# Norms through a constant matrix, single tiles in the first stage, and narrow work between pieces of a product

## The chip, the core and the metric

The kernel runs on one core of a Trainium2 chip. The metric is the device time of one execution: 1261.98 us is the median of three runs (1261.39 to 1262.31). TensorE multiplies matrices into PSUM. VectorE (DVE), ScalarE (ACT) and GpSimd (POOL) do elementwise work. SyncE (SP) issues most transfers.

## The reference

One layer for 320 rows (256 of a prompt, 64 of a running stream), width 2048, in float32:

```
h = RMSNorm(x);  z = h @ w_in            # 2048 -> 1024 q, 128 k, 128 v, 1024 u, 1024 v of the gate
q, k = per-head RMSNorm;  a = windowed attention(q, k, v), 16 heads, bias table, sinks
s = u * (W_s RMSNorm(gelu(zv)) + b), u = gelu(zu)
x = x + concat(RMSNorm(a), RMSNorm(s)) @ w_out       # 2048 -> 2048
y = x + square(relu(RMSNorm(x) @ w_up)) @ w_down      # 2048 -> 8192 -> 2048
```

## The kernel before

Activations lie transposed: 128 features on the partitions, the 320 rows as columns (`T`), so a product takes 128 x 128 blocks of weights as stationary and 320 columns as moving operand. To keep float32 accuracy each operand is split into two fp32r halves, and three passes are added: `w_hi` with `XH`, `w_hi` with `XL`, `w_lo` with `XH`. ScalarE copies a loaded piece of weights into `w_hi` (L125), VectorE subtracts to get `w_lo` (L126). A piece holds 4 tiles of 128 rows by 256 columns, 512 KB, and gives 24 "wide" matmuls (L136). A product is 256 output columns: four pieces for 2048 rows, 96 wide matmuls, into one of two accumulators (`acc`, `ps_acc` with two buffers). The whole program has 8160 wide matmuls. `w_raw` has three buffers in `wp`; from `w_out` on it has seven, in the pool `wf`, which is opened where the pool `at` (attention's tiles) is closed (L455) and takes its memory. `w_hi` and `w_lo` have three buffers each.

A norm's factor is applied after the product, at the eviction from PSUM, so a product can start before its norm is known. The factor is made by `rstd_rows` and `spread`: squares are added up over the tiles, three f32 matmuls sum over the partitions (L158; an f32 matmul runs as two halves in the trace), VectorE adds eps, GpSimd takes the power, three f32 matmuls spread the factors over the partitions (L169) and VectorE copies them out.

The first stage (`products` with `first`) computes two products side by side, keys and values (`kv_ps`, in `acc`) and the first queries (`q0_ps`), as x and weights arrive: single tiles of 128 rows for tiles 0 to 3, then three blocks of four. Each step loads x, splits it into `XH` and `XL` (L178, L179), and loads and splits two weight blocks; only the first four tiles are pinned to program order. Then come three products of queries, four of v with attention's ten units (`attend`) between, four of u, and `w_out` in two halves of eight products (half 0 over attention's output `AH`, `AL`, half 1 over the gate's), and the feed-forward part. The order on each engine is set by a scheduler from program order and its own view of when things are ready; `tc.issue_after` puts an instruction behind another, `keep_in_program_order` pins it. SP's loads follow each other in program order (`load`); small transfers in `between` (the bias) go four at a time behind a load.

Of the kernel before, what the change touches and what calls it, by code (L numbers as in the profile page):

```python
# [29 lines left out]
def hymba_step_kernel(ctx: ExitStack, tc: tile.TileContext, i, o):  # L30
# [47 lines left out]
    inv_dm = const.tile([P, 1], F32, name="inv_dm")  # L78
    nc.vector.memset(inv_dm, 1.0 / DM)
    inv_1k = const.tile([P, 1], F32, name="inv_1k")  # L80
    nc.vector.memset(inv_1k, 1.0 / 1024)
    hone = const.tile([P, 2], F32, name="hone")
# [3 lines left out]
    hsel = const.tile([P, 2], F32, name="hsel")  # L86
    nc.vector.memset(hsel, 0.0)
    nc.vector.memset(hsel[0:HD, 0:1], 1.0 / HD)
    nc.vector.memset(hsel[HD:P, 1:2], 1.0 / HD)


    loads, between, steps = [], [], []
# [8 lines left out]
    def chunks(n, first):  # L101
        if first:
            return [(a, 1) for a in range(4)] + [(a, 4) for a in range(4, n, 4)]
        return [(a, 4) for a in range(0, n, 4)]

    def products(w, k0, nk, jobs, rh, rl, first=None, deep=None):


        wv = w.rearrange("(kt p) n -> p kt n", p=P)
        steps.clear()  # L110
        for a, n in chunks(nk, first is not None):
            if first is not None:
                first(a, n)
                if a % 4 == 0:
                    ahead = blk("w_first", [P, len(jobs), 4, 256])
            for j, (c0, ps) in enumerate(jobs):
                if first is not None:
                    raw = ahead[:, j, a % 4:a % 4 + n]
                else:
                    raw = (deep or wp).tile([P, 4, 256], F32, name="w_raw", tag="w_raw")  # L120
                hi = wp.tile([P, 4, 256], F32R, name="w_hi", tag="w_hi", bufs=3)
                lo = wp.tile([P, 4, 256], F32R, name="w_lo", tag="w_lo", bufs=3)
                load(raw[:, :n], wv[:, k0 + a:k0 + a + n, c0:c0 + 256])
                pin = tc.keep_in_program_order if first is not None and a < 4 else lambda ins: ins
                high = pin(nc.scalar.activation(out=hi[:, :n], in_=raw[:, :n], func=AF.Copy))  # L125
                low = pin(nc.vector.tensor_tensor(out=lo[:, :n], in0=raw[:, :n], in1=hi[:, :n].bitcast(F32),  # L126
                                                  op=ALU.subtract))
                tail = isinstance(ps, list) and a + n == nk
                kgs = [(k, g) for g in range(2) for k in range(n)] if tail else [(k, g) for k in range(n) for g in range(2)]
                passes = [(w_, r_, x) for x, (w_, r_) in enumerate(((hi, rh), (hi, rl), (lo, rh)))]  # L130

                for (k, g), (w_, r_, x) in [(kg, p_) for p_ in passes for kg in kgs] if first is not None else \
                        [(kg, p_) for kg in kgs for p_ in passes]:
                    kk = a + k
                    out = ps[g][:, 0:T] if isinstance(ps, list) else ps[:, g, 0:T]
                    mm = nc.tensor.matmul(out=out, lhsT=w_[:, k, g * P:(g + 1) * P], rhs=r_(kk),  # L136
                                          start=(kk == 0 and x == 0), stop=(kk == nk - 1 and x == 2))
                steps.append((high.ins, low.ins, mm.ins))

    def sums(name):  # L140

        t = sm.tile([P, TP], F32, name=name, tag="ssq", bufs=2)
        nc.gpsimd.memset(t[:, T:TP], 0.0)
        return t
# [4 lines left out]
    def product(w, k0, nk, c0, rh, rl, deep=None, apart=False):  # L149
        ps = [misc(), misc()] if apart else acc_tile()  # L150
        products(w, k0, nk, [(c0, ps)], rh, rl, deep=deep)
        return ps

    def rstd_rows(sq, weight, eps, h=1):

        st = misc()
        for t in range(3):
            nc.tensor.matmul(out=st[:, t * h:t * h + h], lhsT=sq[:, t * P:(t + 1) * P], rhs=weight, start=True, stop=True)  # L158
        r = sm.tile([P, 3 * h], F32, name="r_rows", tag="r_rows")
        nc.vector.tensor_scalar(out=r, in0=st[:, 0:3 * h], scalar1=eps, scalar2=None, op0=ALU.add)  # L160
        rs = sm.tile([P, 3 * h], F32, name="rs_rows", tag="rs_rows")
        nc.gpsimd.tensor_tensor(out=rs, in0=r, in1=nhalf[:, 0:3 * h], op=ALU.pow)
        return rs

    def spread(rs, name):
# [5 lines left out]
        out = sm.tile([P, T], F32, name=name, tag="rstd_b", bufs=2)  # L171
        nc.vector.tensor_copy(out=out, in_=bc[:, 0:T])
        return out

# [9 lines left out]
    def load_x(a, n):  # L184
        load(xT[:, a:a + n], xv[:, a:a + n])
        for k in range(a, a + n):
            split(xT[:, k], g_mix[:, k:k + 1], XH[:, k], XL[:, k], pinned=a < 4)
# [8 lines left out]
    products(w_in, 0, KT, [(1024, kv_ps), (0, q0_ps)], xh, xl, first=load_x)  # L196

    kvx = blk("kvx", [P, 1152])
    kn = kvx[:, 0:448]
    vT = kvx[:, 448:768]  # L200
    rkx = kvx[:, 768:1152].rearrange("p (t c) -> p t c", t=3)
# [13 lines left out]
    nc.sync.dma_start(out=sgb.rearrange("p g i -> p (g i)"), in_=i["sgu_b"].to_broadcast([P, 1024]))  # L215
    wsT = at.tile([P, 8, P], F32, name="wsT", bufs=1)
    nc.sync.dma_start(out=wsT, in_=i["sgu_wT"])
    nc.gpsimd.memset(wsT[HD:P, :, 0:HD], 0.0)
# [3 lines left out]
    b_ps = misc()  # L222
    with tc.issue_after(steps[9][2]):
        nc.tensor.matmul(out=b_ps[0:16, 0:255], lhsT=tab, rhs=oneh, start=True, stop=True)
    b_row = sm.tile([16, 255], F32, name="b_row", tag="w1", bufs=3)
    nc.vector.tensor_copy(out=b_row, in_=b_ps[0:16, 0:255])
    b_dram = dram.tile([16, 15, 255], F32, name="b_dram")
    nc.gpsimd.dma_start(out=b_dram, in_=b_row[:, None, :].to_broadcast([16, 15, 255]))
# [8 lines left out]


    ssq2 = sm.tile([P, 2, T], F32, name="ssq2", tag="w2", bufs=4)
    for k in range(0, KT, 2):  # L240
        sq = sm.tile([P, 2, T], F32, name="sq2", tag="w2", bufs=4) if k else ssq2
        with tc.issue_after(steps[9][0]):
            nc.scalar.activation(out=sq, in_=xT[:, k:k + 2], func=AF.Square)
# [3 lines left out]
    nc.vector.tensor_tensor(out=ssq[:, 0:T], in0=ssq2[:, 0], in1=ssq2[:, 1], op=ALU.add)  # L247

    rx = spread(rstd_rows(ssq, inv_dm, EPS), "rx")


    zk = sm.tile([P, T], F32, name="zk", tag="w2", bufs=4)
    nc.vector.tensor_tensor(out=zk, in0=kv_ps[:, 0, 0:T], in1=rx, op=ALU.mult)
    nc.vector.tensor_tensor(out=vT, in0=kv_ps[:, 1, 0:T], in1=rx, op=ALU.mult)
    sq = sums("ksq")
    nc.scalar.activation(out=sq[:, 0:T], in_=zk, func=AF.Square)
    rk = rstd_rows(sq, hsel, EPS, 2)
# [3 lines left out]
    def queries(g, q_ps):  # L261
# [6 lines left out]
        nc.scalar.activation(out=sq, in_=qg, func=AF.Square)  # L268
        st = misc()
        for b in range(5):  # L270
            nc.tensor.matmul(out=st[:, 2 * b:2 * b + 2], lhsT=sq[:, b].rearrange("p a t -> p (a t)"), rhs=hone,  # L271
                             start=True, stop=True)
# [30 lines left out]
    for g in range(1, 4):  # L303
        queries(g, product(w_in, 0, KT, g * 256, xh, xl))
# [263 lines left out]
```

## Time and profile before

| | us |
|---|---|
| median of the runs | 1261.98 |
| profiled execution | 1262.67 |
| its span, first to last instruction | 1260.9 |
| TensorE busy | 1251.8 |
| VectorE, ScalarE, GpSimd busy | 635.5, 488.9, 104.1 |

"Busy" is the time in which an engine had an instruction running. A matmul's row shows its own length (309 ns), but matmuls overlap, so their pace is read from a stretch of the chain of waits, divided by the count. An instruction's bracket gives the idle time of its engine just before it and what ended that.

### The profile page before, as it was taken

The numbers are of one execution on the slowest core, as the hardware profiler recorded it, in microseconds if no ns is written. First come the engines' busy times: TensorE is split into PE (matmuls) and PEld (weight loads), VectorE is DVE, ScalarE is ACT, GpSimd is POOL, SyncE is SP. The second block draws the span as 40 slices with busy tenths as digits, with TensorE's granted clock in tenths as the row PEclk, the third lists the DMA queues.
The fourth block names the chain that finished last, engine by engine and source line by source line (L and its number), as shares of the span: only waits on it lengthen the run. The fifth ranks groups of instructions, "written<-read, shape, count | busy, mean of one in ns | idle before, by whom it ended". The sixth has DMA issues, their size and how long they took to land.

```text
span 1260.9 us, 20260 instructions
## 1 busy us (share of the span) xinstructions
PE 1251.8 (99%) x8559; PEld 1238.0 (98%) x8559; DVE 635.5 (50%) x731; ACT 488.9 (39%) x636; POOL 104.1 (8%) x100
## 2 busy tenths in 40 slices
PE   8999999999999999999999999999999999999998
PEld 7998899999999999999999999999999999999998
DVE  6547857756864444444444444344444334444443
ACT  7335546523543342233333333344333333343221
POOL 1213443400310000000000000000000000000000
PEclk8999999999999999999999999999999999999999
DMA  9553334644445544445544444555444444544550
GB/s 281 168 141 106 97 115 125 213 142 147 148 143 150 151 149 150 150 149 151 151 150 151 151 150 151 151 150 150 151 150 150 145 149 149 150 152 160 170 168 32
DMA packets 186427, 187.79 MB, mean 149 GB/s; under 512 B 6464, under 2 KB 185856, under 8 KB 186336
## 3 DMA queue, kind: packets, MB, share of 16 engines
q1 hardware_dynamic: 185696, 185.43, 47.5%
q0 software_dynamic: 496, 1.03, 0.4%
q8 instruction: 67, 1.10, 0.4%
q14 instruction: 24, 0.20, 0.0%
q10 hardware_dynamic: 144, 0.03, 0.0%
HBM read 182.91 MB, written 3.32 MB: 148 GB/s over the span
## 4 chain that ended last, share of the span: by engine, by line
PE 98%; DMA 1%; SPq 0%; ACT 0%; POOL 0%; issue 0%; DVE 0%; POOLq 0%
PE acc L136 93%; PE misc L136 1%; PE q_ps L136 1%; DMA xT<-in_xT 1%; PE misc L365 1%; PE misc L371 1%; PE s_ps L327 1%; SPq L99 0%; PE misc L271 0%; PE misc L427 0%; PE misc L158 0%; POOL s L355 0%; PE misc L419 0%; PE misc L169 0%; PE misc L428 0%
## 5 line engine op out<-in xcount | busy, mean ns | idle before, releaser
L126 DVE TENSOR_TENSOR w_lo<-w_raw,w_hi 128x1024 fp32r<-128x1024 f32 x332 | 413.0, 1244 | 458.8 <-ACT w_hi L125 449.8
L125 ACT ACTIVATE w_hi<-w_raw 128x1024 fp32r<-128x1024 f32 x332 | 351.8, 1060 | 714.2 <-PE acc L136 675.7
L136 PE MATMUL acc<-H2H,w_hi 128*128 128x320 f32 x1024 | 316.6, 309 | 0.0
L136 PE MATMUL acc<-H2L,w_hi 128*128 128x320 f32 x1024 | 316.4, 309 | 0.0
L136 PE MATMUL acc<-H2H,w_lo 128*128 128x320 f32 x1024 | 316.4, 309 | 0.0
L136 PE MATMUL acc<-FH,w_hi 128*128 128x320 f32 x992 | 306.5, 309 | 0.0
L136 PE MATMUL acc<-FL,w_hi 128*128 128x320 f32 x992 | 306.5, 309 | 0.0
L136 PE MATMUL acc<-FH,w_lo 128*128 128x320 f32 x992 | 306.5, 309 | 0.0
L136 PEld LDWEIGHTS acc<-H2L,w_hi 128*128 128x128 f32 x1024 | 192.2, 188 | 0.0
L136 PEld LDWEIGHTS acc<-H2H,w_hi 128*128 128x128 f32 x1024 | 192.2, 188 | 0.0
L136 PEld LDWEIGHTS acc<-H2H,w_lo 128*128 128x128 f32 x1024 | 192.2, 188 | 0.0
L136 PEld LDWEIGHTS acc<-FH,w_hi 128*128 128x128 f32 x992 | 186.2, 188 | 0.0
L136 PEld LDWEIGHTS acc<-FL,w_hi 128*128 128x128 f32 x992 | 186.2, 188 | 0.0
L136 PEld LDWEIGHTS acc<-FH,w_lo 128*128 128x128 f32 x992 | 186.2, 188 | 0.0
L136 PE MATMUL acc<-XH,w_hi 128*128 128x320 f32 x384 | 117.8, 318 | 0.3 <-ACT w_hi L125 0.3
L136 PE MATMUL acc<-XL,w_hi 128*128 128x320 f32 x384 | 116.9, 316 | 0.0
L136 PE MATMUL acc<-XH,w_lo 128*128 128x320 f32 x384 | 115.7, 312 | 0.0
L136 PEld LDWEIGHTS acc<-XH,w_hi 128*128 128x128 f32 x384 | 71.9, 191 | 4.2 <-issue 2.1
L136 PEld LDWEIGHTS acc<-XL,w_hi 128*128 128x128 f32 x384 | 72.1, 191 | 1.4 <-issue 1.2
L136 PEld LDWEIGHTS acc<-XH,w_lo 128*128 128x128 f32 x384 | 71.1, 188 | 1.3 <-issue 1.2
L485 DVE SCALAR_TENSOR_TENSOR tf<-acc,r 128x640 f32<-128x640 f32 x32 | 26.4, 825 | 42.7 <-PE acc L136 42.7
L499 DVE TENSOR_TENSOR xT<-xT,acc 128x640 f32<-128x640 f32 x31 | 25.5, 821 | 41.8 <-PE acc L136 41.8
(174 smaller groups left out, 1009.5 us busy)
## 6 DMA issues: line engine op xcount, KB each, us to landing
w_raw<-in_w_up SPq DMA_DIRECT2D x128, 512.0 KB
w_raw<-in_w_down SPq DMA_DIRECT2D x128, 512.0 KB
w_raw<-in_w_in SPq DMA_DIRECT2D x44, 512.0 KB
w_raw<-in_w_out SPq DMA_DIRECT2D x32, 512.0 KB
w_first<-in_w_in SPq DMA_DIRECT2D x6, 512.0 KB
out_yT<-xT SPq DMA_DIRECT2D x7, 320.0 KB
xT<-in_xT SPq DMA_DIRECT2D x3, 640.0 KB
w_first<-in_w_in SPq DMA_DIRECT2D x8, 128.0 KB
```

Source lines behind the costliest of these rows:

```text
L125: high = pin(nc.scalar.activation(out=hi[:, :n], in_=raw[:, :n], func=AF.Copy))
L126: low = pin(nc.vector.tensor_tensor(out=lo[:, :n], in0=raw[:, :n], in1=hi[:, :n].bitcast(F32), op=ALU.subtract))
L136: mm = nc.tensor.matmul(out=out, lhsT=w_[:, k, g * P:(g + 1) * P], rhs=r_(kk), start=(kk == 0 and x == 0), stop=(kk == nk - 1 and x == 2))
L327: nc.tensor.matmul(out=s_ps[:, p, j * nk:(j + 1) * nk], lhsT=qT[hs, blk_, a:a + 2].rearrange("p a t -> p (a t)"), rhs=kz[hs, kv, k0:k0 + n ...
L365: nc.tensor.transpose(out=pt_ps[0:n, (2 * p + j) * P:(2 * p + j + 1) * P], in_=s[:, p, j, c:c + n], identity=ident)
L371: nc.tensor.matmul(out=o_ps[p * HD:(p + 1) * HD, 0:256], lhsT=v[0:n, kv], rhs=pt[0:n, p * 256:(p + 1) * 256], start=(x == 0), stop=(x == l ...
L485: nc.vector.scalar_tensor_tensor(out=t, in0=ps[:, :, 0:T], scalar=0.0, in1=r2[:, None, :].to_broadcast([P, 2, T]), op0=ALU.max, op1=ALU.mult)
L499: nc.vector.tensor_tensor(out=xT[:, a:a + n], in0=xT[:, a:a + n], in1=p, op=ALU.add)
```

## The change

`rstd` replaces `rstd_rows` and `spread` for four norms (x before `w_in`, the keys, the gate's output, x before the feed-forward part): the sums of squares are split into two halves and multiplied by a constant 128 x 128 matrix (`mean_dm`, `mean_hd`, `mean_1k`), so that every partition gets every row's mean; the inverse root is made on VectorE by an integer first guess and three Newton steps. The v gate's norm and attention's norm stay as they were. The sums of squares of attention's output move into the u products, three tiles at a time, and its `rstd_rows` and `spread` stand in the last of these; their tile `acc_a` (now `sums_rows`) lies in the pool `at`. The first stage takes eight single tiles and then four pairs, with one weight transfer and one split for both products. Narrow work (norms, keys, values) is handed to `products` as functions that run behind a given piece, and the next piece is issued behind the last narrow matmul (`behind`). The transfers of `sgb` and `wsT` go behind the bias, and `b_row` is made after tile 7.

```diff
-    def products(w, k0, nk, jobs, rh, rl, first=None, deep=None):
+    def products(w, k0, nk, c0, ps, rh, rl, deep=None, between_pieces={}):
...
+                    with tc.issue_after(behind) if behind else nullcontext():
+                        mm = nc.tensor.matmul(out=out, lhsT=w_[:, k, g * P:(g + 1) * P], rhs=r_(kk),
+                                              start=(kk == 0 and x == 0), stop=(kk == nk - 1 and x == 2))
+            steps.append((high, low, mm.ins))
+            if a // 4 in between_pieces:
+                with tc.issue_after(mm.ins):
+                    between_pieces[a // 4]()
+                    behind = narrow[-1]
...
+    def rstd(acc, mean, eps, out):
+        hl = sm.tile([P, 2, T], F32R, name="n_hl", tag="w2", bufs=4)
+        hi, lo = hl[:, 0], hl[:, 1]
+        nc.scalar.activation(out=hi, in_=acc, func=AF.Copy)
+        nc.vector.tensor_tensor(out=lo, in0=acc, in1=hi.bitcast(F32), op=ALU.subtract)
+        ps = misc()
+        nc.tensor.matmul(out=ps[:, 0:T], lhsT=mean, rhs=hi, start=True, stop=False)
+        narrow.append(nc.tensor.matmul(out=ps[:, 0:T], lhsT=mean, rhs=lo, start=False, stop=True).ins)
...
+        nc.vector.tensor_scalar(out=out.bitcast(I32), in0=x.bitcast(I32), scalar1=-0.5, scalar2=float(0x5F3759DF),
+                                op0=ALU.mult, op1=ALU.add)
+        for _ in range(3):
+            nc.vector.tensor_tensor(out=t, in0=out, in1=out, op=ALU.mult)
+            nc.vector.scalar_tensor_tensor(out=t, in0=t, scalar=-0.5, in1=x, op0=ALU.mult, op1=ALU.mult)
+            nc.vector.scalar_tensor_tensor(out=out, in0=t, scalar=1.5, in1=out, op0=ALU.add, op1=ALU.mult)
...
-    products(w_in, 0, KT, [(1024, kv_ps), (0, q0_ps)], xh, xl, first=load_x)
+    for a, n in [(a, 1) for a in range(8)] + [(a, 2) for a in range(8, KT, 2)]:
...
+        load(xT[:, a:a + n], xv[:, a:a + n])
+        for k in range(n if a else 0):
+            load(raw[:, :, k], wv[:, a + k, 0:2048].rearrange("p (j c) -> p j c", j=2)[:, :, 0:256])
+        for k in range(a, a + n):
+            split(xT[:, k], g_mix[:, k:k + 1], XH[:, k], XL[:, k], pinned=True)
...
+            high, low = halves(raw, hi, lo, pinned=True)
...
+    q1_ps = product(w_in, 0, KT, 256, xh, xl, between_pieces={0: lambda: rstd(ssq, mean_dm, EPS, rx)})
...
+    q2_ps = product(w_in, 0, KT, 512, xh, xl,
+                    between_pieces={0: first_norms, 1: lambda: norm_q(1, q1_sq[0]), 2: keys})
...
+    q2_sq = evict_q(2, q2_ps)
+    q3_ps = product(w_in, 0, KT, 768, xh, xl, between_pieces={0: lambda: norm_q(2, q2_sq)})
+    norm_q(3, evict_q(3, q3_ps))
...
+    def sums_rows(name):
+        t = at.tile([P, TP], F32, name=name, tag="ssq_rows", bufs=1)
...
-                add_square(acc_a, ao[:, a], a == 0)
-                split(ao[:, a], g_oa[:, a:a + 1], AH[:, a], AL[:, a])
+                split(ao[:, a], g_oa[:, a:a + 1], AH[:, a], AL[:, a])
+        for x, a in enumerate(range(3 * g, min(3 * g + 3, 8))):
+            with tc.issue_after(steps[x][0]):
+                add_square(acc_a, ao[:, a], a == 0)
+        if g == 3:
+            with tc.issue_after(steps[0][0]), tc.issue_after(steps[0][1]):
+                rm_a = spread(rstd_rows(acc_a, inv_1k, EPS), rstd_b("rm_a"))
```

On ScalarE, in the first stage, before: `XH` and `w_hi` of tiles 2 and 3, and then the first block of four.

```order
L178 ACTIVATE XH<-xT,cols 128x320
L125 ACTIVATE w_hi<-w_first 128x256 x2
L178 ACTIVATE XH<-xT,cols 128x320
L125 ACTIVATE w_hi<-w_first 128x256
L178 ACTIVATE XH<-xT,cols 128x320
L125 ACTIVATE w_hi<-w_first 128x256
L178 ACTIVATE XH<-xT,cols 128x320 x3
L125 ACTIVATE w_hi<-w_first 128x1024 x2
```

The same place now, from tile 6 to the second pair.

```order
L199 ACTIVATE XH<-xT,cols 128x320
L108 ACTIVATE w_hi<-w_first 128x2x256
L199 ACTIVATE XH<-xT,cols 128x320
L108 ACTIVATE w_hi<-w_first 128x2x256
L199 ACTIVATE XH<-xT,cols 128x320 x2
L108 ACTIVATE w_hi<-w_first 128x1024
L199 ACTIVATE XH<-xT,cols 128x320 x2
L286 ACTIVATE ssq_445<-xT 128x640
```

Before, an `XH` of the block of four stood ahead of tile 3's second `w_hi`; now each tile's `w_hi` follows its own `XH`.

On TensorE, at the sums of the third product's queries (`hone`, `norm_q`), before; the rows around them are the fourth product's.

```order
L136 MATMUL acc<-XH,w_hi 128x320
L136 MATMUL acc<-XL,w_hi 128x320
L271 MATMUL misc<-hone,qsq 128x2 x5
L136 MATMUL acc<-XH,w_lo 128x320
L136 MATMUL acc<-XH,w_hi 128x320
```

And now, at the end of the third product (`acc<-XH` rows): scores (`s_ps`) of units 0 and 1, the sums of `norm_q(2)` (`hone`), and the fourth product's second piece.

```order
L133 MATMUL acc<-XL,w_hi 128x320
L133 MATMUL acc<-XH,w_lo 128x320
L383 MATMUL s_ps<-kzv,qT 128x64 x5
L309 MATMUL misc<-hone,qsq 128x2 x5
L133 MATMUL acc<-XH,w_hi 128x320
```

The sums stood alone among the fourth product's matmuls; they now stand behind scores of two units, directly at the end of the third.

On TensorE, around attention's sums (`acc_a`), before:

```order
L136 MATMUL acc<-AH,w_lo 128x320
L136 MATMUL acc<-AH,w_hi 128x320
L158 MATMUL misc<-inv_1k,acc_a 128x1 x3
L136 MATMUL acc<-AL,w_hi 128x320
L136 MATMUL acc<-AH,w_lo 128x320
```

And now; `acc<-XH` is the last product of u, `acc<-AH` the first of `w_out`.

```order
L133 MATMUL acc<-XL,w_hi 128x320
L133 MATMUL acc<-XH,w_lo 128x320
L156 MATMUL misc<-inv_1k,acc_a 128x1 x3
L188 MATMUL misc<-ident,rs_rows 128x128 x2
L188 MATMUL misc<-ident,rs_rows 128x64
L133 MATMUL acc<-AH,w_hi 128x320
L133 MATMUL acc<-AL,w_hi 128x320
```

The sums stood inside `w_out`'s first product, 42 wide matmuls ahead of their spread (L169); they now stand ahead of `w_out`, and the spread (L188) directly behind them.

## Rows read from the trace of the kernel before

**Rows 1.** The page: the span, each engine's busy time with its share and count.

```profile
span 1260.9 us, 20260 instructions
PE 1251.8 (99%) x8559; PEld 1238.0 (98%) x8559; DVE 635.5 (50%) x731; ACT 488.9 (39%) x636; POOL 104.1 (8%) x100
```

**Rows 2.** Who waited for whom, TensorE only: us in total, times, longest.

```profile
PE q_ps L136 <- ACT w_hi L125: 4.0, 2, 3.3
...
PE acc L136 <- ACT w_hi L125: 0.3, 1, 0.3
PE misc L365 <- POOL s L355: 0.2, 1, 0.2
```

**Rows 3.** The chain of work that ended last: start us, length us, what, count (halves for f32 matmuls).

```profile
26.34 0.53 PE misc L224 x2
...
41.44 0.56 PE misc L158 x6
...
47.09 0.61 PE misc L169 x6
...
89.89 0.59 PE s_ps L327 x8
...
369.11 874.34 PE acc L136 x5961
```

**Rows 4.** The timeline of the first stage: start us, length us, engine, line, operation, out<-in, count, and in brackets the idle time before it and what ended it.

```profile
4.21 0.56 PE L136 MATMUL acc<-XH,w_hi 128*128 128x320 f32 x2
...
5.71 0.56 PE L136 MATMUL q_ps<-XH,w_hi 128*128 128x320 f32 x2 [0.66 <-ACT w_hi L125]
...
11.10 0.46 PE L136 MATMUL acc<-XH,w_lo 128*128 128x320 f32 x2
13.96 0.56 ACT L178 ACTIVATE XH<-xT,cols 128x320 fp32r<-128x320 f32 x1 [4.33 <-DMA xT<-in_xT]
...
14.43 0.40 ACT L125 ACTIVATE w_hi<-w_first 128x256 fp32r<-128x256 f32 x1
...
14.88 0.90 PE L136 MATMUL q_ps<-XH,w_hi 128*128 128x320 f32 x2 [3.33 <-ACT w_hi L125]
...
21.49 1.34 PE L136 MATMUL q_ps<-XH,w_hi 128*128 128x320 f32 x8
...
40.98 0.31 PE L136 MATMUL acc<-XH,w_hi 128*128 128x320 f32 x1
```

**Rows 5.** Three stretches of the first stage: length, busy time (count) of TensorE, its weight loads, VectorE, ScalarE and GpSimd, granted clock as a share of full speed, mean busy share of the DMA engines, GB/s.

```profile
4.21:6.84 2.63, 1.97 (x13) 1.72 (x12) 1.57 (x5) 1.59 (x4) 1.12 (x3) 1.00 0.91 264
6.84:11.56 4.72, 4.71 (x33) 4.45 (x31) 2.82 (x7) 2.18 (x6) 0.00 (x0) 1.00 0.97 304
14.88:21.49 6.61, 6.27 (x23) 5.87 (x23) 6.17 (x10) 6.61 (x12) 0.00 (x0) 0.51 1.09 357
```

**Rows 6.** Groups of instructions by line and shape: count, busy us, mean ns of one, idle time before.

```profile
L126 DVE TENSOR_TENSOR w_lo<-w_raw,w_hi 128x1024 fp32r<-128x1024 f32 x332 | 413.0, 1244 | 458.8 <-ACT w_hi L125 449.8
...
L179 DVE SCALAR_TENSOR_TENSOR XL<-xT,cols,XH 128x320 fp32r<-128x320 f32 x16 | 8.2, 545 | 7.3 <-ACT XH L178 7.1
...
L397 DVE TENSOR_SCALAR gc<-gc 128x640 f32<-128x640 f32 x8 | 3.9, 490 | 0.8 <-ACT gc L396 0.8
...
L336 DVE SCALAR_TENSOR_TENSOR s<-s_ps,rq,bias 128x64 f32<-128x64 f32 x8 | 1.8, 277 | 0.4 <-POOL rq L275 0.4
...
L263 DVE TENSOR_TENSOR qT<-q_ps,rx 128x640 f32<-128x640 f32 x1 | 0.8, 814 | 0.0
L160 DVE TENSOR_SCALAR r_rows<-misc 128x3 f32<-128x3 f32 x5 | 0.8, 153 | 2.9 <-PE misc L158 2.9
...
L247 DVE TENSOR_TENSOR ssq<-ssq 128x320 f32<-128x320 f32 x1 | 0.5, 472 | 0.0
...
L125 ACT ACTIVATE w_hi<-w_raw 128x1024 fp32r<-128x1024 f32 x332 | 351.8, 1060 | 714.2 <-PE acc L136 675.7 <-issue 22.5 <-DMA w_raw<-in_w_in 7.7
...
L268 ACT ACTIVATE qsq<-qT 128x640 f32<-128x640 f32 x4 | 3.0, 740 | 0.7 <-DVE qT L263 0.7
...
L162 POOL TENSOR_TENSOR rs_rows<-r_rows,nhalf 128x3 f32<-128x3 f32 x5 | 4.9, 985 | 51.2 <-DVE r_rows L160 51.2
```

**Rows 7.** The timeline of SP's queue and of the instructions that used what it loaded (columns as in rows 4), and one piece of the chain.

```profile
1.19 0.89 SPq L99 DMA_DIRECT2D w_first<-in_w_in  x2
...
3.76 0.40 ACT L125 ACTIVATE w_hi<-w_first 128x256 fp32r<-128x256 f32 x1
...
31.82 2.60 SPq L99 DMA_DIRECT2D bias<-b_dram  x4
...
34.46 0.44 SPq L99 DMA_DIRECT2D w_raw<-in_w_in  x1
...
38.41 1.06 ACT L125 ACTIVATE w_hi<-w_raw 128x1024 fp32r<-128x1024 f32 x1 [4.38 <-DMA w_raw<-in_w_in]
...
40.51 0.39 SPq L99 DMA_DIRECT2D w_raw<-in_w_in  x1
...
46.44 1.06 ACT L125 ACTIVATE w_hi<-w_raw 128x1024 fp32r<-128x1024 f32 x1 [3.30 <-DMA w_raw<-in_w_in]
...
223.45 96.02 SPq L99 DMA_DIRECT2D w_raw<-in_w_out  x31
...
241.22 0.56 PE misc L158 x6
```

More of the change, by code (lines that the diff above doesn't have):

```diff
@@ L85, in hymba_step_kernel @@
     nc.vector.memset(hone[HD:P, 1:2], 1.0)
[L86 to L92, printed above, removed]
+    loads, between, steps, narrow = [], [], [], []
     def load(out, in_):
@@ L99, in load, with halves @@
                 loads.append(nc.sync.dma_start(out=o_, in_=i_))
[L101 to L104, printed above, removed]
-    def products(w, k0, nk, jobs, rh, rl, first=None, deep=None):
+    def halves(raw, hi, lo, pinned=False):
+        pin = tc.keep_in_program_order if pinned else lambda ins: ins
+        return (pin(nc.scalar.activation(out=hi, in_=raw, func=AF.Copy)).ins,
+                pin(nc.vector.tensor_tensor(out=lo, in0=raw, in1=hi.bitcast(F32), op=ALU.subtract)).ins)
@@ L109, in products, with w_tiles @@
+    def w_tiles():
+        return (wp.tile([P, 4, 256], F32R, name="w_hi", tag="w_hi", bufs=3),
+                wp.tile([P, 4, 256], F32R, name="w_lo", tag="w_lo", bufs=3))
+    def products(w, k0, nk, c0, ps, rh, rl, deep=None, between_pieces={}):
         wv = w.rearrange("(kt p) n -> p kt n", p=P)
+        behind = None
         steps.clear()
[L111 to L134, printed above, removed]
-                    out = ps[g][:, 0:T] if isinstance(ps, list) else ps[:, g, 0:T]
-                    mm = nc.tensor.matmul(out=out, lhsT=w_[:, k, g * P:(g + 1) * P], rhs=r_(kk),
-                                          start=(kk == 0 and x == 0), stop=(kk == nk - 1 and x == 2))
-                steps.append((high.ins, low.ins, mm.ins))
@@ new lines, in products @@
+        for a in range(0, nk, 4):
+            raw = (deep or wp).tile([P, 4, 256], F32, name="w_raw", tag="w_raw")
+            hi, lo = w_tiles()
+            load(raw, wv[:, k0 + a:k0 + a + 4, c0:c0 + 256])
+            high, low = halves(raw, hi, lo)
+            tail = isinstance(ps, list) and a + 4 == nk
+            for k, g in [(k, g) for g in range(2) for k in range(4)] if tail else [(k, g) for k in range(4) for g in range(2)]:
+                kk = a + k
+                for x, (w_, r_) in enumerate(((hi, rh), (hi, rl), (lo, rh))):
+                    out = ps[g][:, 0:T] if isinstance(ps, list) else ps[:, g, 0:T]
+                    with tc.issue_after(behind) if behind else nullcontext():
[6 more added lines that the diff above has]
+                    behind = narrow[-1]
@@ L152, in product, with rstd_rows @@
         return ps
-    def rstd_rows(sq, weight, eps, h=1):
+    def rstd_rows(sq, weight, eps):
         st = misc()
         for t in range(3):
[L158 to L162, printed above, removed]
-        return rs
@@ L167, in spread @@
+    def spread(rs, out):
         bc = misc()
@@ L195, in hymba_step_kernel @@
     q0_ps = ps_sc.tile([P, 2, 512], F32, name="q0_ps", tag="s_ps")
-    products(w_in, 0, KT, [(1024, kv_ps), (0, q0_ps)], xh, xl, first=load_x)
-    kvx = blk("kvx", [P, 1152])
+    wv = w_in.rearrange("(kt p) n -> p kt n", p=P)
+    for a, n in [(a, 1) for a in range(8)] + [(a, 2) for a in range(8, KT, 2)]:
+        if a % 4 == 0:
+            ahead = blk("w_first", [P, 2, 4, 256])
+        raw = ahead[:, :, a % 4:a % 4 + n]
+        load(xT[:, a:a + n], xv[:, a:a + n])
[3 more added lines that the diff above has]
+            split(xT[:, k], g_mix[:, k:k + 1], XH[:, k], XL[:, k], pinned=True)
+        hi, lo = [t.rearrange("p (j k) c -> p j k c", j=2)[:, :, 0:n] for t in w_tiles()]
+        if a:
+            high, low = halves(raw, hi, lo, pinned=True)
+        else:
+            for j in range(2):
+                load(raw[:, j, 0], wv[:, 0, j * 1024:j * 1024 + 256])
+                high, low = halves(raw[:, j, 0], hi[:, j, 0], lo[:, j, 0], pinned=True)
+        for x, (w_, r_) in enumerate(((hi, xh), (hi, xl), (lo, xh))):
+            for j, k, g in [(j, k, g) for j in range(2) for k in range(n) for g in range(2)]:
+                ps = q0_ps if j == 0 else kv_ps
+                mm = nc.tensor.matmul(out=ps[:, g, 0:T], lhsT=w_[:, j, k, g * P:(g + 1) * P], rhs=r_(a + k),
+                                      start=(a + k == 0 and x == 0), stop=(a + k == KT - 1 and x == 2))
+        steps.append((high, low, mm.ins))
+        if a == 5:
+            b_ps = misc()
+            with tc.issue_after(mm.ins):
+                nc.tensor.matmul(out=b_ps[0:16, 0:255], lhsT=tab, rhs=oneh, start=True, stop=True)
+        if a == 7:
+            b_row = sm.tile([16, 255], F32, name="b_row", tag="w1", bufs=3)
+            with tc.issue_after(low):
+                nc.vector.tensor_copy(out=b_row, in_=b_ps[0:16, 0:255])
+            b_dram = dram.tile([16, 15, 255], F32, name="b_dram")
+            nc.gpsimd.dma_start(out=b_dram, in_=b_row[:, None, :].to_broadcast([16, 15, 255]))
+    kvx = blk("kvx", [P, 768])
     kn = kvx[:, 0:448]
     vT = kvx[:, 448:768]
-    rkx = kvx[:, 768:1152].rearrange("p (t c) -> p t c", t=3)
     nc.sync.dma_start(out=kn[:, 256:384], in_=i["ckT"])
@@ L236, in hymba_step_kernel @@
                 between.append((bias[hh * HD:(hh + 1) * HD, p, j], src))
+    between.append((sgb.rearrange("p g i -> p (g i)"), i["sgu_b"].to_broadcast([P, 1024])))
+    between.append((wsT, i["sgu_wT"]))
     ssq2 = sm.tile([P, 2, T], F32, name="ssq2", tag="w2", bufs=4)
@@ L246, in hymba_step_kernel, with evict_q @@
     ssq = sums("ssq")
[L247 to L257, printed above, removed]
+    nc.vector.tensor_tensor(out=ssq, in0=ssq2[:, 0], in1=ssq2[:, 1], op=ALU.add)
+    rx, rk = rstd_b("rx"), rstd_b("rk")
     rq = at.tile([P, 4, 10], F32, name="rq", bufs=1)
-    def queries(g, q_ps):
+    def evict_q(g, q_ps):
         qg = qT[:, :, 2 * g:2 * g + 2]
@@ new lines, in hymba_step_kernel, with first_norms @@
+    q1_ps = product(w_in, 0, KT, 256, xh, xl, between_pieces={0: lambda: rstd(ssq, mean_dm, EPS, rx)})
+    zk = sm.tile([P, T], F32, name="zk", tag="w2", bufs=4)
+    nc.vector.tensor_tensor(out=zk, in0=kv_ps[:, 0, 0:T], in1=rx, op=ALU.mult)
+    nc.vector.tensor_tensor(out=vT, in0=kv_ps[:, 1, 0:T], in1=rx, op=ALU.mult)
+    ksq = sums("ksq")
+    nc.scalar.activation(out=ksq, in_=zk, func=AF.Square)
+    q0_sq = evict_q(0, q0_ps)
+    q1_sq = []
+    def first_norms():
+        rstd(ksq, mean_hd, EPS, rk)
+        norm_q(0, q0_sq)
+        q1_sq.append(evict_q(1, q1_ps))
@@ L438, in hymba_step_kernel @@
         if g == 0:
-            acc_a = sums("acc_a")
+            acc_a = sums_rows("acc_a")
             AH, AL = blk("AH", [P, 8, T], F32R), blk("AL", [P, 8, T], F32R)
@@ L460, in hymba_step_kernel @@
     acc_x = sums("acc_x")
-    for half, (hi, lo, acc) in enumerate(((AH, AL, acc_a), (SH, SL, acc_s))):
-        rm = spread(rstd_rows(acc, inv_1k, EPS), f"rm{half}")
+    rm_s = rstd_b("rm_s")
+    for half, (hi, lo, rm) in enumerate(((AH, AL, rm_a), (SH, SL, rm_s))):
         for g in range(8):
@@ L468, in hymba_step_kernel @@
             nc.vector.tensor_tensor(out=x1, in0=x1, in1=t, op=ALU.add)
+            if half == 0 and g == 2:
+                rstd(acc_s, mean_1k, EPS, rm_s)
             if half == 1:
```

105 lines of the change are left out of this document (53 added, 52 removed).

## The prediction

> **What bounds the kernel now.** I read the page first: TensorE is busy for 1251.8 of 1260.9 us, and the other engines half the time or less [rows 1]. Then the waits of TensorE: idle time is short, and 4.0 us of it is one line, the first stage waiting for `w_hi` on ScalarE [rows 2]. Then the chain of waits: from 369.11 on it is one stretch of 5961 wide matmuls in 874.34 us, 146.7 ns each [rows 3]; between wide matmuls stand short matmuls in f32 that cost TensorE as much as anything else does. So a gain can only come from a shorter first stage, from fewer short matmuls, or from the end, and the change leaves the end alone; each new wait of TensorE is paid in full. The sum is made against the profiled execution, 1262.67 us (span 1260.9 and 1.8 around it), 0.7 above the median of the runs, 1261.98.
>
> **First stage.** Its 192 wide matmuls are worth 192 x 0.1467 = 28.2 us. They run from 4.21 to 40.98 [rows 4], with the `oneh` product (0.53 [rows 3]) inside: 36.8 - 0.5 - 28.2 = 8.1 us lost. The timeline shows where. TensorE runs out at 11.5 because ScalarE's next instruction is `XH` of the first block of four tiles, whose 640 KB land at 13.96; the `w_hi` that TensorE wants stands behind it. It resumes at 14.88, and until 21.49 the granted clock is 0.51 of full speed, the lower of its two levels [rows 4, 5]: 22 matmuls in 6.27 us that are worth 3.23, so 3.0 us for the clock after 3.3 us of idle time.
>
> After the change the order on ScalarE is x, w, x, w for eight single tiles, so no instruction waits for four tiles of x at once. Transfers kept a pace of one tile (420 KB) per 1.4 us at 304 GB/s between 6.84 and 11.56, and 357 GB/s later [rows 5]; TensorE needs 12 x 0.1467 = 1.76 us per tile. VectorE needs per tile an `XL` (0.545) and a `w_lo` of 512 elements (half of 1244 ns), 1.17 us, and ScalarE an `XH` (0.56) and half a `w_hi` of 1060, 1.09 [rows 4, 6]: all below 1.76. What stays lost is the start: 0.7 us until the second half of `w_first` is there (4.21 to 6.84), and some 0.2 us in each of the first three tiles, because one `w_hi` now covers both products and waits for 256 KB. I keep 1.3 us of the loss: gain 6.8 us. Bounds: 7.4 (only the 0.7 stays) and 3.8 (TensorE, fed by single tiles, drops to the lower clock as it did at 14.88, 3.0 us).
>
> The Trainium skill, DMA: Bandwidth & Descriptors, Rules for kernel authors, speaks against this part: it wants small transfers joined into large ones, since each has a fixed part of about 2 us. Were the 8 added transfers paid one after the other, that would be 16 us lost by this estimate. The trace does not agree that it is paid serially: SP issued transfers 0.48 us apart and their bytes flowed on.
>
> **The norms.** Four pairs go: three sums (six halves, 0.56 us) and three spreads (0.61), 1.17 us per norm [rows 3]. Each is replaced by two matmuls of 320 columns at the wide rate, 0.29 us. 4 x 0.88 = 3.5 us off TensorE; all are in its line, so all of it counts. The eleven VectorE instructions in place of one copy are some 0.45 us each (0.472 for a sum of this size, half of 0.490 for a tensor_scalar [rows 6]), 5 us. VectorE is half idle and TensorE meanwhile works on the next product, so they cost nothing where the second accumulator is free: `rx` is followed by the eviction of `kv_ps`, whose accumulator the third product needs 10.6 us (72 matmuls) later; eleven instructions, two weight splits of 1.24 and two evictions come to 8.5, but the splits wait for TensorE's release of `w_hi`, so it is close, and the sums that feed `rx` come as close. I allow 0.4 us of waits for all norms (0 to 2).
>
> **Narrow work between pieces.** `behind` makes the product's next piece wait for the narrow matmul. On the third such place this bites. The order of TensorE shows the scores of units 0 and 1 and then `norm_q(2)` right behind the last matmuls of the third product, and piece 1 of the fourth behind them. `norm_q(2)` needs that product's eviction (0.81 us) and its square (0.74); the scores of unit 1 need the four score evictions of unit 0 on VectorE, 4 x 0.28, behind the same eviction [rows 6]. So TensorE resumes its scores 0.1 + 0.8 + 1.1 = 2.0 us after the product's end, and has 3 score matmuls (0.45, at 0.59 per four [rows 3]) to do meanwhile: 1.5 us idle that before did not exist, there the same matmuls stood among wide ones. Bounds 0.5 (only eviction and square less the scores) and 3.0 (a weight split of 1.06 or 1.24 in front of either).
>
> **Attention's sums, and the loads behind them.** `acc_a` now lives in `at`, and its only matmul reader, the sums of `rstd_rows` (L156), is emitted behind the last u product. The order of TensorE has it and L188 behind all of that product's matmuls, with nothing between and nothing of `w_out` before them. `at` is closed there, and `wf`, with the seven buffers of `w_out`'s loads, takes its place. So the first load of `w_out`, and SP's queue with everything behind it, waits for TensorE to reach L156. Before, SP issued these loads from 223.45 on, 18 us ahead of the sums at 241.22 [rows 7], while the u product ran. This is a new wait with nothing to hide it, since no wide matmul is left that has its weights. From the end of L156, T: the load lands at T+4.0 (issued 34.46, its `w_hi` began at 38.41 [rows 7]); `w_hi` 1.06; two matmuls; the third needs `w_lo`, 1.24 [rows 6], so steady work resumes at T+6.4 with 0.1 for the semaphores. Inside lie the spreads (0.61, after 0.15 on VectorE and 0.99 on GpSimd) and two matmuls (0.29), which are work in both kernels: 5.5 us idle. Bounds of the landing: 2.6 us (128 KB, issued 1.19, used at 3.76) and 5.9 (issued 40.51, used at 46.44) [rows 7]: 4.1 to 7.4. By the fit in the same page of the Trainium skill (Anatomy of one DMA), 512 KB would take an estimated 3.2 us, and the stall would be 4.7.
>
> Then the clock. After 3.3 us of idle time it was at 0.51 for 6.6 us and cost 3.0. Here TensorE is idle for 5.5 of 6.4 us, in two stretches with the spreads between; I expect the drop, and take 2.4, since part of the low stretch may lie in the idle time (0 to 3.3). The Trainium skill, TensorE: Matmul & The Clock Gate, Part 1, says that the throttled clock is the default and only sustained work lifts it; by that rule the few spreads don't hold it up, and the cost is nearer 3.0. The trace's 14.88 to 21.49 agrees.
>
> The earlier rows of `bias` in the queue (b_row after tile 7, where SP waited until 31.82 before [rows 7]) and `sgb` and `wsT` behind the next product's first load move transfers that TensorE does not wait for: nothing. The sums of squares of attention move on ScalarE and GpSimd, which have room: nothing.
>
> **Sum.** -6.8 - 3.5 + 0.4 + 1.5 + 5.5 + 2.4 = -0.5 us: the gain of the first stage and the norms is handed back at `w_out`. 1261.98 - 0.5 = 1261.5 us.
>
> **Rivals.** *The clock holds at w_out* (faster): the spreads break the idle time, and the load lands sooner, by 1.0 us, as it has the engines to itself. For it: the gap of 0.66 us at 5.71 cost no clock; against it: 3.3 us did. -0.5 - 2.4 - 1.0 = -3.9: 1258.1. *The loads come late* (slower than before): seven loads of 512 KB are let go at once and share 16 engines, so that the first lands at 5.9 as at 40.51, and the low clock costs its full 3.0: -0.5 + 1.9 + 0.6 = +2.0, 1264.0. It turns slower than before from a landing 0.5 us later than I take. Against it: SP issues them 0.44 us apart in one queue, and at 40.51 eight small `bias` transfers stood around. *The loads don't wait* (the change does what it says): the stall and its clock stay away, -0.5 - 7.9 = -8.4: 1253.6. Against it stands the order.
>
> **Chances.** Forecast 0.48, clock holds 0.28, loads late 0.18, no stall 0.06. A measurement of this kernel tells 0.2% (2.5 us) from no change: below 1259.5 is faster, above 1264.5 slower. Faster are the fourth and most of the second, 0.30 together; slower are half of the third (the landing at its bound and the third product's or the first stage's too) and 0.08 of the forecast, where the first stage is at its lower bound: 0.17; same 0.53. Range 1256.5 to 1265.5: it takes in the clock at both ends and the landing from 2.6 to 5.9, and leaves out the no-stall case.
>
> **What would show it.** First matmul of the second product near 34 in place of 40.98, no waits over 1 us before it, granted clock 1.0 up to there: first stage right. Four places with two matmuls of 320 columns: norms right. A TensorE wait of about 1.5 us on `s_ps` or `qsq` at the end of the third product; a wait of about 3 us on `w_hi` and 1 us on `w_lo` right after L188, with the first `w_out` issue on SP just behind L156, and the granted clock near half in the 5 us after. If `w_out`'s loads stand before the end of the u products, or TensorE's idle time there is under 3 us, the forecast is wrong.

## The result, and the profile after

The changed kernel takes 1265.78 us (median of its executions) against 1261.67 for the kernel before, measured beside it: a ratio of 1.0030, 95% interval 1.0023 to 1.0037. It is about 4 us slower. The forecast was 1261.5 with a range up to 1265.5; the result lies just above it.

The trace that came with the result hides this. Its execution took 1261.78 us, the fastest of all; the others that count lie between 1263.1 and 1267.0 (one disturbed run is left out). The mean granted clock of that execution was 0.997; 15 of the 18 others were at 0.994 to 0.996, three at 0.997. In the profiled one the sum of the prediction came out almost exactly: its span is 1259.8 against 1260.9 [rows 1], 1.1 less where the sum had 0.5 less. First the page (as in rows 1) and the waits of TensorE (as in rows 2) of this execution:

```profile
span 1259.8 us, 20220 instructions
PE 1248.1 (99%) x8519; PEld 1233.0 (98%) x8519; DVE 658.5 (52%) x767; ACT 489.7 (39%) x638; POOL 97.2 (8%) x97
```

```profile
PE acc L133 <- ACT w_hi L108: 2.2, 1, 2.2
PE misc L188 <- POOL rs_rows L160: 1.4, 1, 1.4
...
PE s_ps L383 <- DVE s L392: 1.1, 1, 1.1
PE q_ps L235 <- ACT w_hi L108: 0.7, 1, 0.7
PE misc L421 <- ACT ao L430: 0.7, 2, 0.4
PE acc L133 <- DVE w_lo L109: 0.4, 1, 0.4
PE misc L427 <- DVE pt L423: 0.3, 1, 0.3
```

The 3.3 us of the first stage [rows 2] are gone. In their place stand 4.0 us in three pieces at `w_out` (lines 133, 188 and 133 again), 1.1 us on `s_ps` at the end of the third product, and 1.0 in attention (lines 421 and 427), which no step of the prediction had.

The timeline, TensorE, with the two instructions that released it and SP's issue of `w_out`'s loads (columns as in rows 4):

```profile
7.59 0.56 PE L235 MATMUL q_ps<-XH,w_hi 128*128 128x320 f32 x2 [0.73 <-ACT w_hi L108]
...
34.81 0.31 PE L133 MATMUL acc<-XH,w_hi 128*128 128x320 f32 x1
...
72.48 0.44 PE L383 MATMUL s_ps<-kzv,qT 64*128 64x64 f32 x4 [1.10 <-DVE s L392]
72.85 1.28 PE L309 MATMUL misc<-hone,qsq 128*128 128x2 f32 x10
...
234.28 0.72 PE L156 MATMUL misc<-inv_1k,acc_a 128*128 128x1 f32 x6
235.09 9.19 SPq L103 DMA_DIRECT2D w_raw<-in_w_out  x9
236.39 1.25 PE L188 MATMUL misc<-ident,rs_rows 128*128 128x128 f32 x6 [1.38 <-POOL rs_rows L160]
238.72 1.06 ACT L108 ACTIVATE w_hi<-w_raw 128x1024 fp32r<-128x1024 f32 x1 [2.59 <-DMA w_raw<-in_w_out]
239.83 0.64 PE L133 MATMUL acc<-AH,w_hi 128*128 128x320 f32 x1 [2.19 <-ACT w_hi L108]
239.81 1.23 DVE L109 TENSOR_TENSOR w_lo<-w_raw,w_hi 128x1024 fp32r<-128x1024 f32 x1 [1.64 <-ACT w_hi L108]
241.09 0.64 PE L133 MATMUL acc<-AH,w_lo 128*128 128x320 f32 x1 [0.36 <-DVE w_lo L109]
```

The second product begins at 34.81 in place of 40.98 [rows 4]. At `w_out` the prediction can be followed row by row: SP issues 0.1 us behind L156, the load lands 3.6 us later, `w_hi` takes 1.06, the third matmul waits for `w_lo`, and TensorE is steady again at 241.09, 6.1 us behind the end of L156 (forecast 6.4). The granted clock of that place (columns: stretch, length, TensorE's busy time and count, granted clock, DMA share, GB/s):

```profile
236.86:243.72 6.86, 4.31 (x17) 0.51 1.00 330
```

So one execution agrees with the sum, and the median one costs 4 us more, in most cases at a lower mean clock. That was left to explain.

### The profile page after: what moved, and what is told of

Same layout as the page of the kernel before. It is cut to its first block, busy times and chain, and to the rows that moved or that the text cites. A ratio compares the mean times of both kernels' runs of the same rounds, so it can differ in the third digit from the quotient of the medians.

```text
span 1259.8 us, 20220 instructions
## 1 busy us (share of the span) xinstructions
PE 1248.1 (99%) x8519; PEld 1233.0 (98%) x8519; DVE 658.5 (52%) x767; ACT 489.7 (39%) x638; POOL 97.2 (8%) x97
## 4 chain that ended last, share of the span: by engine, by line
PE 95%; DMA 2%; DVE 1%; SPq 1%; ACT 1%; issue 0%; ACTq 0%
PE acc L133 90%; PE misc L133 1%; DMA w_raw<-in_w_in 1%; SPq L103 1%; PE s_ps L383 1%; PE misc L427 1%; PE misc L421 1%; DMA b_dram<-b_row 1%; PE q_ps L235 0%; PE acc L235 0%; DMA w_first<-in_w_in 0%; PE misc L309 0%; ACT w_hi L108 0%; PE misc L489 0%; DMA w_raw<-in_w_out 0%
## 5 line engine op out<-in xcount | busy, mean ns | idle before, releaser
L133 PE MATMUL acc<-XH,w_hi 128*128 128x320 f32 x352 | 110.1, 313 | 0.1
L133 PE MATMUL acc<-XH,w_lo 128*128 128x320 f32 x352 | 110.0, 312 | 0.0
L133 PE MATMUL acc<-XL,w_hi 128*128 128x320 f32 x352 | 110.0, 312 | 0.0
L133 PEld LDWEIGHTS acc<-XH,w_hi 128*128 128x128 f32 x352 | 66.2, 188 | 1.6 <-issue 1.2
L133 PEld LDWEIGHTS acc<-XH,w_lo 128*128 128x128 f32 x352 | 66.1, 188 | 1.6 <-issue 1.4
L133 PEld LDWEIGHTS acc<-XL,w_hi 128*128 128x128 f32 x352 | 66.1, 188 | 1.2 <-issue 1.2
```

## Experiments

**The changed kernel again.** Nothing edited. Expected:

> The changed kernel, unaltered, timed and profiled again. The profile at hand is of its fastest execution (1261.78 us, mean granted clock 0.997); the median is 1265.78, at clocks from 0.994 to 0.997. Theory A (the sum is right for that one execution, but in a typical one the granted clock falls for longer behind the wait for w_out's weights): again a median near 1265.5, and in a profile of 1264 to 1267 us the stretch below full clock around w_out is longer than the 6.7 us of the first profile, or dips come after it. Theory B (the first stage, fed by single tiles, runs into the lower clock in most executions, and the profile shows the exception): the second product's first matmul at 37 to 39 us in place of 34.8. Theory C (neither; waits elsewhere vary): first stage and w_out as in the first profile, and 3 to 4 us of new waits of TensorE in attention.

Measured: 1264.63 us, ratio to before 1.0022 (1.0013 to 1.0031). This time the profiled execution is a longer one, near the median of the result: 1265.28 us, span 1263.1, clock 0.995. Its second product begins at 34.08, so theory B does not explain this execution. `w_out` is as in the first profile, but behind the wait on `s_ps`, ahead of `w_out`, stands a second dip of the clock, which none of the three theories had there. Windows of it, columns as above, and the timeline:

```profile
72.00:73.00 1.00, 0.61 (x7) 1.00 0.00 0
73.00:74.00 1.00, 1.00 (x8) 0.61 0.06 16
74.00:75.00 1.00, 1.00 (x6) 0.50 0.36 52
...
79.00:80.00 1.00, 1.00 (x5) 0.50 0.00 0
80.00:81.00 1.00, 1.00 (x8) 0.98 0.00 0
```

```profile
72.39 0.44 PE L383 MATMUL s_ps<-kzv,qT 64*128 64x64 f32 x4 [1.10 <-DVE s L392]
72.75 1.91 PE L309 MATMUL misc<-hone,qsq 128*128 128x2 f32 x10
74.52 0.61 PE L133 MATMUL acc<-XH,w_hi 128*128 128x320 f32 x1
...
237.35 0.72 PE L156 MATMUL misc<-inv_1k,acc_a 128*128 128x1 f32 x6
```

The same 1.10 us wait at the same place: in the first profile the clock stayed at 1.00, here it is at the lower level from about 73.2 to 80.0 (from the shares of the first and last window). The scores behind the wait stand 0.1 us sooner than in the first profile, and L156 3.1 us later (237.35 against 234.28). That is the missing time of this execution. It does not explain every one: three executions of the result's set had the mean clock of the first profile, 0.997, and still took 1264.8 to 1266.1 us; no trace shows what they lost.

**The sums' tile in another pool**, which takes away what `w_out`'s loads wait for; run in two sets:

```diff
     def sums_rows(name):
-        t = at.tile([P, TP], F32, name=name, tag="ssq_rows", bufs=1)
+        t = sm.tile([P, TP], F32, name=name, tag="ssq_rows", bufs=1)
```

> The changed kernel with the tile of the three sums (acc_v, acc_a) in pool sm instead of at, so that w_out's loads no longer have to wait for TensorE's sums of acc_a. By the prediction's terms 5.5 us of idle time and 2.4 of low clock go: about 8 us faster than the changed kernel's profile, TensorE's wait on w_hi at w_out below 0.5 us, the granted clock at 1.0 from 30 us to the end. Theory A (the clock behind that wait is what makes a typical execution 4 us longer): 10 to 12 us below the changed kernel's median, 1254 to 1256. Theory B (first stage): 7 to 8 below, 1258, and the clock stays under 1.0 in the first 40 us. Rival (the loads wait for something else too, or TensorE's wait is for something else): 0 to 2 us.

> The changed kernel with the sums' tile in pool sm once more, to see in more executions whether the wait at the third product's end (1.1 us, still in it) lowers the clock. Theory D: some of the executions show a mean granted clock below 0.999 and take 2 to 3 us longer than those at 1.0. Rival E (the dip at 73 us needs the later wait at w_out, or something else that this kernel no longer has): all executions at 0.999 or 1.0, as the five before, and 1256 to 1258.5.

Measured: 1257.27 (ratio to before 0.9968, 0.9956 to 0.9980) and 1258.21 (0.9974, 0.9965 to 0.9983), the first 7.4 us below the changed kernel measured beside it. That is near the prediction's own 5.5 + 2.4; the 10 to 12 us of theory A are not there. The wait at `w_out` is gone altogether: SP issues its loads from 219.86 on in place of 235.09, `AH` matmuls follow L156 at once, and L188 stands among them. So it was the wait for L156 that held the loads back. In the first set all five executions had a mean clock of 0.999 or 1.000, and its profile has the 1.10 us wait on `s_ps` without a dip. In the second, eleven executions, they spread as theory D says, though by more than its 2 to 3 us: the three fastest (1256.5 to 1256.7) at 0.999 to 1.000, the two slowest (1260.0 and 1261.5) at 0.997. Its profile has the dip behind the wait on `s_ps`, about half as long as in the second profile of the changed kernel. That stretch there and here (columns as in rows 5; the granted clocks are the 0.83 and the 0.91):

```profile
60.00:80.00 20.00, 18.90 (x113) 18.22 (x113) 11.12 (x29) 5.39 (x13) 7.47 (x8) 0.83 0.42 123
```

```profile
60.00:80.00 20.00, 18.90 (x125) 18.22 (x125) 12.35 (x31) 5.85 (x14) 8.19 (x8) 0.91 0.45 124
```

Rival E of the second set falls: the dip comes without any wait at `w_out`.

**The narrow work one piece later**, with the edit above:

```diff
-    q3_ps = product(w_in, 0, KT, 768, xh, xl, between_pieces={0: lambda: norm_q(2, q2_sq)})
+    q3_ps = product(w_in, 0, KT, 768, xh, xl, between_pieces={1: lambda: norm_q(2, q2_sq)})
```

> As the run before, and norm_q(2) behind the second piece of the fourth product instead of the first, so that eight tiles' worth of matmuls less stand between... that is: one piece of wide matmuls more may run before the narrow matmuls that wait for the third product's eviction. By the prediction's term for the third product's end, 1.1 us (its wait of TensorE on s_ps in the profile) goes: 1.0 to 1.5 us faster than the run before. Rival (the scores of the first two units, which wait for the same eviction, still stand behind the last matmul of the third product): no difference, and the wait on s_ps is still there.

Measured: 1258.07 (0.9976, 0.9968 to 0.9985), no gain over the edit above alone, where 1.0 to 1.5 us were expected. The wait only moved: the scores of two units stand in one block, and behind them TensorE waits for a weight split that ScalarE has not reached. The clock dips there too:

```profile
73.95 0.66 PE L383 MATMUL s_ps<-kzv,qT 64*128 64x64 f32 x8
75.39 0.42 PE L133 MATMUL acc<-XH,w_hi 128*128 128x320 f32 x1 [0.77 <-ACT w_hi L108]
```

```profile
77.00:78.00 1.00, 1.00 (x6) 0.59 0.81 253
78.00:79.00 1.00, 1.00 (x6) 0.50 0.82 260
```

**norm_q(2) free**, without a wait of the next pieces behind it, in the changed kernel otherwise untouched:

```diff
-    q3_ps = product(w_in, 0, KT, 768, xh, xl, between_pieces={0: lambda: norm_q(2, q2_sq)})
+    norm_q(2, q2_sq)
+    q3_ps = product(w_in, 0, KT, 768, xh, xl)
```

> The changed kernel with norm_q(2) called before the fourth product and no wait of that product's pieces behind it, so that the scores and norm_q(2) stand among wide matmuls again; the wait at w_out stays. Theory D (the second profile of the changed kernel showed it: behind the 1.1 us wait on s_ps at the third product's end the granted clock is at 0.50 from 73.4 to 80.0 us, which costs 3.1 us, and this happens in most executions): the 1.1 us and most of the 3.1 go, 3 to 4 us faster than the changed kernel, 1261 to 1262, and the granted clock is 1.0 from 66 to 90 us. Rival E (only the idle time goes; the clock falls anyway, since the short matmuls of the scores and of norm_q(2) are still there): 1 us faster, and a dip after 72 us in the profile.

Measured: 1261.94 (1.0004, 0.9995 to 1.0013). By the ratios to before, 1.0022 and 1.0030 for the changed kernel's two sets, that is 2.3 to 3.3 us below it. Windows of 20 us from 60 to 220 are busy to 20.00 at a clock of 1.00; the wait on `s_ps` is gone, and so are the 1.0 us of waits in attention. So the idle time that went is 2.1 us, not 1.1, and 0.2 to 1.2 is left for the clock. Rival E falls as far as this profile goes: the scores and the sums of `norm_q(2)` are still there, among wide matmuls, and no dip follows. The wait at `w_out` is still there (2.6, 1.4 and 0.4 us), with its dip.

This profile also has a longer wait earlier, of 1.5 us, on the squares of the keys (`ksq`), and the clock stays at 1.00 behind it. Its row, and the stretches with that wait, with the place of the old wait on `s_ps`, and with the scores and sums, which now begin at 80.3:

```profile
PE acc L133 <- ACT ksq L332: 1.5, 1, 1.5
```

```profile
40.00:60.00 20.00, 18.50 (x129) 18.26 (x128) 15.44 (x26) 7.14 (x9) 3.29 (x4) 1.00 0.70 210
60.00:80.00 20.00, 20.00 (x142) 19.95 (x141) 12.89 (x24) 5.82 (x6) 5.93 (x7) 1.00 0.43 123
80.00:100.00 20.00, 20.00 (x145) 18.84 (x144) 11.22 (x31) 7.76 (x23) 5.13 (x4) 1.00 0.47 139
```

**Both edits**, the sums in `sm` and `norm_q(2)` free:

> Both: the sums' tile in pool sm and norm_q(2) free. Theory D: no stall over 0.8 us after 10 us and a clock of 1.0 in all executions; as fast as the best executions of the run with the sums in sm (1256.35) less 1.1: 1255 to 1256.5. Rival (the narrow work among the wide matmuls now makes other waits): 1257 or more, with new waits of TensorE between 40 and 80 us.

Measured: 1253.95 (0.9944, 0.9930 to 0.9958), 7.6 us below before, 4.3 below the kernel with only the sums in `sm` beside it, and by the ratios 10 to 11 below the changed kernel; better than expected, since the waits in attention go as well. All five executions are at a clock of 1.0, and the list of waits of TensorE has one row, ahead of the first load:

```profile
span 1252.5 us, 20224 instructions
PE 1247.7 (100%) x8519; PEld 1234.0 (99%) x8519; DVE 656.6 (52%) x767; ACT 490.4 (39%) x638; POOL 100.0 (8%) x97
```

```profile
PE misc L78 <- DVE hone L91: 1.3, 1, 1.3
```

```profile
233.30 0.72 PE L156 MATMUL misc<-inv_1k,acc_a 128*128 128x1 f32 x6
233.88 0.39 PE L133 MATMUL acc<-AH,w_hi 128*128 128x320 f32 x1
...
238.22 0.78 PE L188 MATMUL misc<-ident,rs_rows 128*128 128x128 f32 x6
```

**The new first stage alone, in the kernel before**, and then with the change's order of loads. The first keeps the old places of `b_row`, `sgb` and `wsT`; the second moves them as the change does:

```diff
+        if a == 7:
+            b_row = sm.tile([16, 255], F32, name="b_row", tag="w1", bufs=3)
...
-    nc.sync.dma_start(out=wsT, in_=i["sgu_wT"])
+    between.append((wsT, i["sgu_wT"]))
```

> The kernel before with the new first stage alone (single tiles, then pairs; both halves of the weights split by one instruction). The first profile of the changed kernel gained 6.2 us to the second product's first matmul. Theory A: 5.5 to 6.5 us faster than before, about 1255.5, granted clock 1.0 throughout. Theory B (a typical execution loses the clock in the first stage): 2 to 3 us faster only, with a mean granted clock at 0.997 or less. Rival (what the first stage gains is lost again at the norm of x, which now comes sooner than its transfers and squares): 0 to 3 us faster, at full clock, with a wait of TensorE right behind the first stage.

> The kernel before with the new first stage and with the change's order of loads (b_row behind tile 7 and its store, sgb and wsT behind the first loads of the next product). The new first stage alone gained 2.8 us where the changed kernel's profile showed 6.2, and its trace has TensorE waiting 1.6 us for w_hi and 0.7 for w_lo at 40 us, with the w_raw of the second product landing at 39.4 behind wsT and b_dram. If that is why (theory F: what I priced at nothing, the moved loads, is what lets the first stage keep its gain): these waits go, 2 to 2.5 us faster than with the first stage alone, 1256.5 to 1257. Rival G (the load stands late because the first stage itself takes the bandwidth, and the buffers of w_raw come free no earlier): the same time as the first stage alone, within 0.7, waits still there.

Measured: 1259.07 (0.9983, 0.9975 to 0.9992) with the first stage alone, and 1256.28 (0.9962, 0.9949 to 0.9974) with the loads moved: 2.8 and 5.3 us below before. The 5.5 to 6.5 us that theory A expected of the first are not there; its rival had the size, 0 to 3 us, and a wait soon behind the first stage, but another cause. In the first kernel SP stands at `bias` until 32.98, since `b_dram` is written late; the next `w_raw` is issued at 35.62, and the second product, which now wants it, waits. With the loads moved `bias` goes out at 25.87. SP's queue and TensorE, of the first and then of the second:

```profile
32.98 2.60 SPq L99 DMA_DIRECT2D bias<-b_dram  x4
35.62 0.44 SPq L99 DMA_DIRECT2D w_raw<-in_w_in  x1
...
40.47 0.42 PE L136 MATMUL acc<-XH,w_hi 128*128 128x320 f32 x1 [1.61 <-ACT w_hi L125]
41.73 0.41 PE L136 MATMUL acc<-XH,w_lo 128*128 128x320 f32 x1 [0.70 <-DVE w_lo L126]
```

```profile
25.87 2.60 SPq L99 DMA_DIRECT2D bias<-b_dram  x4
28.51 0.44 SPq L99 DMA_DIRECT2D w_raw<-in_w_in  x1
```

Theory F holds, rival G falls. Of the first kernel's eleven executions five had a mean clock of 0.998 or 0.999 and took 1260.4 to 1262.1, the others were at 1.0 and took 1258.2 to 1259.1; where the clock fell in the five was not traced.

## Why the prediction was wrong, step by step

The step that failed is the third product's end, "Narrow work between pieces". It had 1.5 us, bounds 0.5 to 3.0, and counted idle time alone. The idle time was within the bounds (1.10), the place and the releaser were right. What it lacked is the clock: behind that wait TensorE ran at the lower level for some 6.8 us, 3.1 us lost, in the second profile; for about half of that in one with the sums in `sm`; and not at all in the first profile and in the other one with the sums in `sm`. I had priced the clock only at `w_out` and in the first stage, from two rows: 0.66 us of idle time cost none, 3.3 did [rows 4]. A wait of 1.5 us lies between the two, so it wanted a bound of 0 to 3.0 for its clock, as the others had, and got none. The same edit brought 1.0 us of waits in attention, which go when `norm_q(2)` is set free; why the later units wait less then was not traced. The step was worth 1.1 + 3.1 + 1.0 = 5.2 us in the second profile, not 1.5.

The medians, which take in every execution, put it lower and spread the miss over more steps. Setting `norm_q(2)` free is worth 2.3 to 3.3 us in the changed kernel and 4.3 with the sums in `sm` (forecast 1.5); the first stage with its loads gives 5.3 (forecast 6.8), the norms with the smaller edits 2.3 (forecast 3.1), and `w_out` costs 7.4 to 8.0 (forecast 7.9). So of the 4.3 us by which the forecast was too low, 0.8 to 2.8 belong to the third product's end, 1.5 to the first stage and 0.8 to the norms. That the first profile's span came out within 0.6 of the sum was partly luck: `w_out` was 1.5 cheaper there, the first stage and the third product's end 0.6 dearer each.

The other steps, each with what it measured:

- *First stage*, forecast -6.8: -6.2 and -6.9 in the two profiles (34.81 and 34.08 against 40.98). The size was right there. In three other profiles with the changed first stage the second product begins only at 35.96 to 36.31, since TensorE starts at the slower pace shown in the last section: 4.7 to 5.0 less than before. "Transfers that TensorE does not wait for: nothing" was wrong as a reading: with the old order of loads half the gain is lost, 2.8 us where 5.3 are to be had. When a stage is shortened, the loads that just held before are the next thing late.
- *Norms*, forecast -3.5 and +0.4 of waits: between the profiles of the last two kernels above, both edits and the first stage with its loads, whose second products begin within 0.1 us of each other (36.31 and 36.38), the span shrinks by 3.8 us (1256.3 to 1252.5), with 0.2 us of waits in the one and none in the other; by the medians it is 2.3. This takes in the smaller edits that the two don't share, and the profiled execution of the second is the slowest of its five (1258.1); which of the two figures is nearer stays open. In the other kernels' profiles the waits of the norms were between nothing and 1.5 us.
- *w_out*, forecast 5.5 + 2.4 = 7.9: from L156 to the start of the long last stretch of the chain it is 130.51 us in the first profile and 124.11 in the kernel with both edits: 6.4 us. The mechanism was right to the row, and its three rivals fall: the clock dropped, the loads waited, and they were not late. The idle time was smaller, 4.0 for 5.5, partly because the spreads inside it took 1.25 in place of 0.61. I had taken 4.0 us for the landing, and the row shows 3.6. The Trainium skill's fit (DMA: Bandwidth & Descriptors, Anatomy of one DMA) gave an estimated 3.2 for 512 KB; the page gives that fit for transfers issued from GpSimd, and these are SyncE's.

The last rows of the chain on which the 6.4 rests, of the first profile and of the kernel with both edits:

```profile
364.79 877.65 PE acc L133 x5984
```

```profile
357.41 877.65 PE acc L133 x5984
```

With the third step mended, the sum is -6.9 - 3.5 + 0.4 + 5.2 + 6.4 = +1.6 us for the execution of the second profile (the norms' two terms as forecast); its span is 2.2 longer than before.

## What to carry to other kernels

A wait of TensorE can have two prices, its idle time and the lower clock behind it; where only shorter and longer idle times were seen, the second price belongs into the bounds. One execution's trace can be the lucky one: hold its time against the median and the clocks of all runs before reading it. And it matters in which pool a tile lies, not only how large it is: here the late reader of one tile in a pool that closes held back every load into the pool that takes its memory.

## What the hardware showed beside that

The same 1.10 us wait at the same place lowered the clock in one execution and not in another (72.39 and 72.48 above). Its length alone does not decide: the 1.5 us on `ksq` left the clock at 1.00. What decides it stays open, and so does in how many executions of the changed kernel it fell: their mean clocks go from 0.994 to 0.997, where the profile without the dip has 0.997 and the one with it 0.995.

The granted clock in the profile doesn't show the start. In the kernel with both edits the first matmuls follow each other at the pace of the lower level, 0.73 us for two that overlap against 0.46 later, until about 10.3, while the column reads 1.00; in the kernel before two took 0.73 at 15.58, under a granted clock of 0.51. In the changed kernel's two profiles only the first pair was slower (0.72 and 0.83). It costs some 2 us: the second product begins at 36.31 there, at 34.08 in the second profile. The slow start stands in four of the nine profiles with single tiles in the first stage, so it may be part of what the executions at a mean clock of 0.997 lost; in three of the four kernels whose profile has it, that execution is the longest among those of the same mean clock. No trace of the changed kernel itself shows it.

```profile
9.21 0.73 PE L235 MATMUL q_ps<-XL,w_hi 128*128 128x320 f32 x2
...
10.94 0.46 PE L235 MATMUL q_ps<-XH,w_hi 128*128 128x320 f32 x2
```
